# Scaling a GEMM's inputs one block earlier, and two more Winograd quads in that block

## The chip, the cores and the metric

One core of a Trainium2 chip. The metric is the device time of one execution in microseconds (us); the median of the runs counts.

## The reference

One transformer block on 256 tokens of width 2048, all in float32: a gated feed-forward stage (ffn), a mixer, and a second ffn.

```python
def _swiglu(x, w_gate, w_up, w_down):
    return (jax.nn.silu(x @ w_gate) * (x @ w_up)) @ w_down
...
        f = _swiglu(_rmsnorm(h, ln_ffn1_pre[l]), ffn1_gate[l], ffn1_up[l], ffn1_down[l])
        h = h + MACARON_WEIGHT * _rmsnorm(f, ln_ffn1_post[l])
        mx = _hybrid_mixer(_rmsnorm(h, ln_mix_pre[l]), ...)
        h = h + _rmsnorm(mx, ln_mix_post[l])
        f = _swiglu(_rmsnorm(h, ln_ffn2_pre[l]), ffn2_gate[l], ffn2_up[l], ffn2_down[l])
        h = h + MACARON_WEIGHT * _rmsnorm(f, ln_ffn2_post[l])
```

The feed-forward width is 5632, so gate and up are 2048 x 5632 each and down is 5632 x 2048. `_rmsnorm` divides each token's row by its root mean square: one factor per token (a row factor) and one gain per column.

## The kernel before

**Numbers in two halves.** Each float32 operand is split in a high half in a reduced format (a cast on ScalarE, ACT) and a low half, the rest (a subtraction on VectorE, DVE). A product is three matmuls (`mm3`, L317): high x high, high x low, low x high. Weights come from memory through SP's queue, two groups of 128 rows at a time (`w32`), and are split into a ring of five buffers (`wH`, `wL`): ACT line L295 and DVE line L296 where the framework orders the work, L373 and L383 where the kernel's own planner does.

**Gate and up.** Both have 11 blocks of 512 columns. Block 0 is made by `gemm_tok`, first gate, then up; the framework's scheduler places its instructions by program order and readiness, with the weight splits put ahead. Up of block 0 is 96 matmuls of 512 columns; its evacuation (`up(h)`: L1010, then a 32 x 32 block transpose, L875) is left to the plan that follows. Blocks 1 to 10 and the down stage are one plan: `Plan.solve` sorts all their operations by modelled times, due times and buffers, and the engines run them in that order. `p.begin` is a node of 12 us that stands for the last stretch of up of block 0; `UNITS` says how many of the 33 large buffers ("units") the plan may count on at its start.

**Pairs and quads.** A block is written as a string in `GATE_UP`. `f` is a pair: two groups of 128 input columns, all tokens, times gate's weights; `l` the same for up; a pair is 12 matmuls. `q` is a quad: two groups of input columns times both gate's and up's weights, by a Winograd form with seven products in place of eight (21 matmuls in place of 24). A quad costs seven VectorE operations on weights: L576 (two columns of 512 at once), L581 and L585 (512), and four low halves L598 (three of 1024, one of 512). It needs sums and differences of the inputs' halves (`sums`: four operations of 256 columns at L441 to L446, a cast at L482, a low half at L486; once for two quads). A block with quads ends in a merge: L640 on ACT, four adds L645, two closings L645, two totals L693 on VectorE.

**Row factors.** `uT` is the transposed input with the column gains, without the row factors `rs`. Block 0 and block 1 of before read `uT`, and their evacuation multiplies by `rs`. Blocks 2 to 10 read `nT`, which has the factors in it. `spread` turns `rs` from one number per partition into a row `rsb`: a copy on VectorE (L1099), a transpose on TensorE (L1101), a copy on ScalarE (L1102), once for each half of the tokens. `normed` then makes `nT` from `uT`, for four groups: join the halves (L1119), scale by `rsb` (L1123), cast the high half (ACT, L1132), subtract for the low half (L1127). In the kernel before these are operations of the plan; two joins run during up of block 0 and the rest during block 1. Block 1 has no quad; blocks 2, 4, 6, 8, 10 have four and blocks 3, 5, 7, 9 three.

**What else stands there.** `setup_mixer` (from `s.after`, first ffn only) loads the mixer's parameter rows by 12 small DMAs on SP and turns them on TensorE.

Of the kernel before, what the change touches and what calls it, by code (L numbers as in the profile page):

```python
# [10 lines left out]
F32 = mybir.dt.float32  # L11
F32R = mybir.dt.float32r
AF = mybir.ActivationFunctionType
ALU = mybir.AluOpType
# [3 lines left out]
P = 128  # L18
# [26 lines left out]
DOWN = ((0, "fffffffffffqfff" "qllqllqllqllqllqllqll", 0),  # L45
        (2, "fqflqfqflqfqflqfqflqfqfqff", TRAIL))
OUT = ((0, "", 0), (1, "fffqfq" "qlqlll", 0), (3, "", TRAIL))
GATE_UP = ["", "ffffffffllllllll"] + ["ffqfqfqlqlll", "fffqffqlqllll", "ffqfqfqlqlll", "fffqffqlqllll", "ffqfqfqlqlll", "fffqffqlqllll", "ffqfqfqlqlll", "fffqffqlqllll", "ffqfqfqlqlll"]
SUMS = (2, 2)
BY_DMA = range(0)  # L50
LAT = dict(PE=0.22, DVE=0.1, ACT=0.17, SP=0.0, POOL=8.0)
AGAIN = dict(PE=0.0, DVE=0.0, ACT=0.0, SP=0.0, POOL=0.0)
UNITS = dict(ffn=25, out=22)
FIFO = dict(pt=4, pm=4, tmp=TB)
SPARE, KEEP, URGENT, HOLD = 3, 4, 8.0, 99
SOON, FETCH, LATEST, BEFORE = 22.0, 22.0, 12.0, 12.0
EARLY = 0.5
NXSPARE = 1
RATE, LEAVE, LAND, ADD, MOVE = 0.28, 1.05, 2.0, 10.0, 12.0

ROWS = [("ln_mix_pre", 16), ("ln_ffn2_pre", 16), ("mu", 26), ("w0", 8), ("a0", 8),
# [5 lines left out]
def cost(eng, n, extra=0.0):  # L67
    return extra + (n / 960 + 0.068 if eng == "DVE" else n / 1200 + 0.095)
# [152 lines left out]
class Block:  # L221
# [99 lines left out]
        nc.tensor.matmul(ps, aL, bH, start=False, stop=stop)  # L321

    def gemm_tok(s, w, c0, at, KT, evac, lead=False, trail=False, xs=None, hold=False,
                 order=None):
        pss = [s.pm.tile([P, 512], F32, tag="mm", name=s.nm("mm")) for _ in range(2)]
        ws = {}

        def do(k, h):
            (wH, wL), (xH, xL) = ws[k], at(k)
            s.mm3(pss[h], xH[:, h * P:h * P + P], xL[:, h * P:h * P + P], wH, wL,  # L330
                  k == 0, k == KT - 1)

        def keep(tiles):
            ws.update((k, (wH, wL)) for k, wH, wL in tiles)

        def both(k0, k1):
            for k2 in order or range(k0, k1, 4):
                keep(s.load_w(w, k2, min(4, k1 - k2), c0, 512))
                for k in range(k2, min(k2 + 4, k1)):
                    do(k, 0)  # L340
                    do(k, 1)

        if trail:
            both(0, KT - TRAIL)
            s.by_half(w, c0, KT - TRAIL, KT, do, keep, lambda h, d: evac(h, d, lambda: pss[h]))
            return
        k0 = 0
        if xs:
            s.head(w, c0, KT, do, keep, xs)
            k0 = KT  # L350
        elif lead:
            s.by_half(w, c0, 0, STAG, do, keep, ready=s.ready)
            s.run()
            k0 = STAG
        both(k0, KT)
        if hold:
            return lambda h: evac(h, pss[h])
        with s.tc.high_priority(offset=BOOST):
            for h in range(2):
                evac(h, pss[h])  # L360
# [60 lines left out]
    def sums(s, T, Td, j, out, own=None, nq=2, used=(), x32=None):  # L421
# [11 lines left out]
            V.tensor_tensor(out=fl(x), in0=xH, in1=xL, op=ALU.add)  # L433

        def second():
            x = tt["x"] if x32 is None else x32[0][0].rearrange(
                "p (a b) t -> p a b t", b=2)[:, :nq]
            a11, a21 = x[:, :, 0, :P], x[:, :, 0, P:]
            a12, a22 = x[:, :, 1, :P], x[:, :, 1, P:]
            f = tt["f"] = s.unit((P, 4, nq, P), F32, "sf")  # L440
            V.scalar_tensor_tensor(out=f[:, 0], in0=a21, scalar=-1.0, in1=a22, op0=ALU.mult,  # L441
                                   op1=ALU.subtract)
            V.scalar_tensor_tensor(out=f[:, 1], in0=f[:, 0], scalar=-1.0, in1=a11,
                                   op0=ALU.mult, op1=ALU.subtract)
            V.tensor_tensor(out=f[:, 2], in0=a11, in1=a21, op=ALU.subtract)
            V.tensor_tensor(out=f[:, 3], in0=a12, in1=f[:, 1], op=ALU.subtract)  # L446

# [541 lines left out]
    def ffn(s, wg, wu, wd, uT, rs, gpost, resid, emit, reload, xs=None):  # L989
# [9 lines left out]
        def turned(b, h, src):  # L999
            if not T1[b]:  # L1000
                T1[b].append(s.unit(p="T1"))
            s.turn(T1[b][0], h, src)
# [5 lines left out]
        def ev_um(b, h, ps):  # L1008
            g = sig[b, h]
            nc.vector.scalar_tensor_tensor(out=g, in0=ps, scalar=rs[h], in1=g, op0=ALU.mult,  # L1010
                                           op1=ALU.mult)

        s.gemm_tok(wg, 0, at, NKD, lambda h, ps: ev_g(0, h, ps), lead=True, xs=xs)
        up = s.gemm_tok(wu, 0, at, NKD, lambda h, ps: (ev_um(0, h, ps), turned(
            0, h, sig[0, h])), hold=True)
        while s.after:
            s.after.pop(0)()
        rb = s.rtmp("rsb")
        s.spread(rs, rb)

        p = s.plan
        p.units = UNITS["ffn"]
# [13 lines left out]
            hTk.append(k)  # L1036
        carry(0, [last], k1)

        uTk = [Tok("unit") for _ in range(2 * len(uT))]
        for k in uTk:  # L1040
            k.of = "unit"
        nT, nTd, nTk, nx = s.normed(uT, rb)
        su, sud, suk = [None] * 4, {}, []

        def need(q):
            j = q // 2
            if j not in sud:
                sud[j], k = s.sums(nT, nTd, j, su, nq=SUMS[j], x32=nx[j])
                suk.extend(k)
            return sud[j]  # L1050

        for b in range(1, nb):
            mul, silu = {}, {}
            k1 = Tok("unit")

            def ev_f(h, d, ap, use, b=b, silu=silu):
                if b == 1:
                    before, mine = p.claim("tmp")
                    n = p.op("ACT", cost("ACT", 512, 0.05), lambda: ev_g(b, h, ap()),
                             [d] + before)  # L1060
                    silu[h] = n, mine
                    use.append(n)
                    return

                def f():
                    sig[b, h] = ap()
                    nc.scalar.activation(out=ap(), in_=ap(), func=AF.Silu)
                silu[h] = p.op("ACT", cost("ACT", 512), f, [d]), use

            def ev_l(h, d, ap, use, b=b, silu=silu, mul=mul, k1=k1):  # L1070
                g, mine = silu[h]

                def mult():
                    nc.vector.tensor_tensor(out=ap(), in0=ap(), in1=sig[b, h], op=ALU.mult)
                if b == 1:
                    m = p.op("DVE", one, lambda: ev_um(b, h, ap()), [d, g])
                    src, mine2 = (lambda: sig[b, h]), mine
                    use.append(m)
                else:
                    m = p.op("DVE", one, mult, [d, g])  # L1080
                    src, mine2 = ap, use
                    mine.append(m)
                t = p.op("DVE", one, lambda: turned(b, h, src()), [m],
                         [k1] if h == 0 else (), chain=f"turn{b}")
                mine2.append(t)
                mul[h] = t
            x, dep = (at, lambda k: None) if b == 1 else (s.T_at(nT), lambda k: nTd[k // 4])
            s.seven(wg, b * 512, wu, b * 512, x, dep, NKD, need, su, GATE_UP[b], ev_f, ev_l, {})
            if b == 1:
                p.release([p.last], uTk)  # L1090
            carry(b, [mul[0], mul[1]], k1)
        p.release([p.last], nTk + suk)
        s.post(wd, s.T_at(hT), NKF, gpost, 0.5, resid, emit, reload, hT, hTd, sm, DOWN, hTk)
# [9 lines left out]

    def normed(s, uT, rb):

        nc, p = s.nc, s.plan
        V = nc.vector
        nT = s.new_T(len(uT))
        fl = lambda t: t.rearrange("p k t -> p (k t)")
        done, toks, own = [], [], {}  # L1110
        rows = p.op("ACT", 2.0, lambda: None, [p.begin])
        for i in range(len(uT)):
            (uH, uL), (nH, nL) = uT[i], nT[i]
            x = {}
            kx, kT = Tok("unit"), [Tok("unit"), Tok("unit")]

            def join(x=x, uH=uH, uL=uL):
                x[0] = s.unit((P, 4, S), F32, "nx")
                V.tensor_tensor(out=fl(x[0]), in0=fl(uH).bitcast(F32), in1=fl(uL).bitcast(F32),  # L1119
                                op=ALU.add)  # L1120

            def scale(x=x):
                V.tensor_tensor(out=x[0], in0=x[0],  # L1123
                                in1=rb.unsqueeze(1).to_broadcast([P, 4, S]), op=ALU.mult)

            def low(x=x, nH=nH, nL=nL):
                V.tensor_tensor(out=fl(nL), in0=fl(x[0]), in1=fl(nH).bitcast(F32),  # L1127
                                op=ALU.subtract)
            n = p.op("DVE", cost("DVE", 1024), join, (), [kx], early=BEFORE - 3.0)
            n = p.op("DVE", cost("DVE", 1024), scale, [n, rows])  # L1130
            n = p.op("ACT", cost("ACT", 1024),
                     lambda x=x, nH=nH: nc.scalar.copy(fl(nH), fl(x[0])), [n], kT)  # L1132
            done.append(p.op("DVE", cost("DVE", 1024), low, [n], (),
                             () if i < len(SUMS) else [kx]))
            toks += kT
            if i < len(SUMS):
                own[i] = x, kx
        return nT, done, toks, own

    def post(s, wd, at, KT, gpost, fac, resid, emit, reload, hT, hTd, sm, plan, hTk=None):  # L1140
        nc = s.nc
# [873 lines left out]
```

## Time and profile before

| | |
|---|---|
| median of 3 runs | 2017.49 us (2016.72 to 2018.85) |
| the profiled execution's own time | 2017.13 us |
| its span, first to last instruction | 2015.4 us |
| TensorE clock granted | 0.998 |
| TensorE busy | 2000.9 us (99%) |
| weight loads into TensorE | 1655.1 us (82%) |
| VectorE busy | 1824.7 us (91%) |
| ScalarE busy | 1192.3 us (59%) |
| GpSimd busy | 327.6 us (16%) |

PE is TensorE, PEld its weight loads, DVE VectorE, ACT ScalarE, POOL GpSimd, SP the queue that issues most loads. In a table of stretches, each engine has its busy us and its number of instructions in brackets. In a timeline a row has start, duration, engine, line, operation, tiles (out<-in), shapes, count, and in brackets the idle time before it with what ended it. Matmul durations overlap (0.39 us each while they start 0.23 apart), and some matmul records can be missing.

The first ffn's gate/up runs from about 7 to 475 us of the span, the mixer from about 700 to 1230, the second ffn's gate/up from about 1310 to 1785.

### The profile page before, as it was taken

The numbers are of one execution on the slowest core, as the hardware profiler recorded it, in microseconds if no ns is written. First come the engines' busy times: TensorE is split into PE (matmuls) and PEld (weight loads), VectorE is DVE, ScalarE is ACT, GpSimd is POOL, SyncE is SP. The second block draws the span as 40 slices with busy tenths as digits, with TensorE's granted clock in tenths as the row PEclk, the third lists the DMA queues.
The fourth block names the chain that finished last, engine by engine and source line by source line (L and its number), as shares of the span: only waits on it lengthen the run. The fifth ranks groups of instructions, "written<-read, shape, count | busy, mean of one in ns | idle before, by whom it ended". The sixth has DMA issues, their size and how long they took to land.

```text
span 2015.4 us, 28684 instructions
## 1 busy us (share of the span) xinstructions
PE 2000.9 (99%) x9957; PEld 1655.1 (82%) x9957; DVE 1824.7 (91%) x2424; ACT 1192.3 (59%) x1586; POOL 327.6 (16%) x673
## 2 busy tenths in 40 slices
PE   9999999999999999999999999999999999999997
PEld 7888888888888888888788788888888888888886
DVE  6999999999999957789689678979999999999997
ACT  7555665556666566685476434665656555566663
POOL 0111211131000123403220111011113111310000
PEclk9999999999999999999999999999999999999999
DMA  7675674667568577757456547666656747665683
GB/s 268 224 241 182 220 242 160 218 213 241 175 203 299 209 212 214 205 175 214 146 173 190 159 168 269 244 216 215 228 198 218 245 142 235 211 228 183 207 294 126
DMA packets 227419, 423.56 MB, mean 210 GB/s; under 512 B 24639, under 2 KB 28105, under 8 KB 227273
## 3 DMA queue, kind: packets, MB, share of 16 engines
q1 hardware_dynamic: 204713, 384.70, 57.9%
q0 software_dynamic: 22272, 36.51, 5.5%
q8 instruction: 78, 1.28, 0.3%
q10 hardware_dynamic: 288, 0.52, 0.1%
q14 instruction: 68, 0.56, 0.1%
HBM read 396.69 MB, written 8.39 MB: 201 GB/s over the span
## 4 chain that ended last, share of the span: by engine, by line
PE 97%; DVE 1%; issue 1%; DMA 0%; ACT 0%; POOLq 0%; POOL 0%; DVEq 0%; ACTq 0%
PE mm L319 27%; PE mm L321 26%; PE mm L320 26%; PE ms L320 5%; PE ms L321 5%; PE ms L319 5%; PE tr L849 1%; PE pA L1733 0%; DVE u L645 0%; PE mc L817 0%; DMA x<-in_x_dram 0%; PE pU L1829 0%; PE pSa L1841 0%; PE pY L1864 0%; PE pT L1900 0%
## 5 line engine op out<-in xcount | busy, mean ns | idle before, releaser
L319 PE MATMUL mm<-wH,xH 128*128 128x512 f32 (+1 forms) x2116 | 825.5, 391 | 0.0
L320 PE MATMUL mm<-wL,xH 128*128 128x512 f32 (+1 forms) x2116 | 821.2, 388 | 0.0
L321 PE MATMUL mm<-wH,xL 128*128 128x512 f32 (+1 forms) x2116 | 821.1, 388 | 0.0
L319 PEld LDWEIGHTS mm<-wH,xH 128*128 128x128 f32 x2116 | 397.4, 188 | 82.1
L321 PEld LDWEIGHTS mm<-wH,xL 128*128 128x128 f32 x2116 | 397.4, 188 | 82.0 <-DVE xL L867 0.2
L373 ACT CAST wH<-w 128x1024 fp32r<-128x1024 f32 x313 | 326.2, 1054 | 231.7 <-PE mm L321 208.1
L320 PEld LDWEIGHTS mm<-wL,xH 128*128 128x128 f32 x2116 | 397.7, 188 | 79.7
L383 DVE TENSOR_TENSOR wL<-w,wH 128x1024 fp32r<-128x1024 f32 x313 | 373.0, 1218 | 18.9 <-ACT wH L373 17.3
L593 ACT CAST wH<-t 128x1024 fp32r<-128x1024 f32 x208 | 219.4, 1055 | 217.0 <-PE mm L321 108.9
L296 DVE TENSOR_TENSOR wL<-w,wH 128x1024 fp32r<-128x1024 f32 (+2 forms) x200 | 236.6, 1192 | 95.7 <-ACT wH L295 94.1
L295 ACT CAST wH<-w 128x1024 fp32r<-128x1024 f32 (+2 forms) x200 | 205.4, 1034 | 170.9 <-PE mm L321 150.7
L892 POOL DMA_DIRECT2D x<-T x352 | 173.1, 499 | 729.8 <-DVE T L875 190.3
L598 DVE TENSOR_TENSOR wL<-t,wH 128x1024 fp32r<-128x1024 f32 x208 | 248.6, 1217 | 0.7 <-ACT wH L593 0.7
L593 ACT CAST wH<-w 128x1024 fp32r<-128x1024 f32 x208 | 168.3, 835 | 56.6 <-PE mm L321 30.0
L598 DVE TENSOR_TENSOR wL<-w,wH 128x1024 fp32r<-128x1024 f32 x208 | 194.5, 951 | 0.3
L576 DVE TENSOR_TENSOR t<-w,w 128x1024 f32<-128x1024 f32 x104 | 126.7, 1218 | 0.0
L320 PE MATMUL ms<-wL,sH 128*128 128x512 f32 x276 | 107.6, 390 | 0.2
L319 PE MATMUL ms<-wH,sH 128*128 128x512 f32 x276 | 107.4, 389 | 0.0
L321 PE MATMUL ms<-wH,sL 128*128 128x512 f32 x276 | 107.4, 389 | 0.0
L585 DVE TENSOR_TENSOR t<-w,t 128x512 f32<-128x512 f32 x104 | 71.8, 690 | 2.6
L581 DVE TENSOR_TENSOR t<-w,t 128x512 f32<-128x512 f32 x104 | 71.3, 686 | 0.6
L645 DVE TENSOR_TENSOR u<-ms,u 128x512 f32<-128x512 f32 x92 | 61.4, 686 | 1.4
(317 smaller groups left out, 2107.8 us busy)
## 6 DMA issues: line engine op xcount, KB each, us to landing
w<-in_w_in_dram SPq DMA_DIRECT2D x128, 512.0 KB
w<-in_ffn_up_dram SPq DMA_DIRECT2D x112, 512.0 KB
w<-in_ffn_gate_dram SPq DMA_DIRECT2D x110, 512.0 KB
w<-in_ffn_down_dram SPq DMA_DIRECT2D x104, 512.0 KB
w<-in_ffn_down_dram SPq DMA_DIRECT2D x144, 256.0 KB
w<-in_ffn_gate_dram SPq DMA_DIRECT2D x132, 256.0 KB
w<-in_ffn_up_dram SPq DMA_DIRECT2D x128, 256.0 KB
w<-in_w_out_dram SPq DMA_DIRECT2D x24, 512.0 KB
```

Of the source, the lines that this page charges most:

```text
L295: s.nc.scalar.copy(vH, v)
L296: s.nc.vector.tensor_tensor(out=vL, in0=v, in1=vH.bitcast(F32), op=ALU.subtract)
L319: nc.tensor.matmul(ps, aH, bH, start=start, stop=False)
L320: nc.tensor.matmul(ps, aH, bL, start=False, stop=False)
L321: nc.tensor.matmul(ps, aL, bH, start=False, stop=stop)
L373: nc.scalar.copy(x["H"], x["v"])
L383: nc.vector.tensor_tensor(out=x["L"], in0=x["v"], in1=x["H"].bitcast(F32), op=ALU.subtract)
L576: V.tensor_tensor(out=v["t13"], in0=v["a"], in1=v["b"][:, :1].to_broadcast([P, 2, 512]), op=ALU.subtract)
L585: V.tensor_tensor(out=v["t24"][:, 1], in0=v["b"][:, 1], in1=v["t24"][:, 0], op=ALU.subtract)
L593: nc.scalar.copy(H, src)
L598: V.tensor_tensor(out=L, in0=src, in1=H.bitcast(F32), op=ALU.subtract)
L892: nc.gpsimd.dma_start(out=x[0][q * 32:q * 32 + 32, i], in_=src[i * 32:i * 32 + 32, q])
```

## The change

Row factors: `spread` and the joins now stand between gate and up of block 0, and `setup_mixer` after them, all ahead of up. Up's loop calls `aside` after each group of four; it writes scale, cast and low of one group of `nT` (`split`). `normed` has no plan operations any more; the plan takes `nT` as ready at `p.begin`, counts on 15 units in place of 25, and gets those of `uT` back at `p.begin` rather than after block 1. Block 1 reads `nT` like the others, with no factors in its evacuation.

Quads: block 1 gets two, and the strings of blocks 2 to 10 start with three, so that these hold 31 in place of 32: 33 per stage, not 32.

```diff
-GATE_UP = ["", "ffffffffllllllll"] + ["ffqfqfqlqlll", "fffqffqlqllll", "ffqfqfqlqlll", "fffqffqlqllll", "ffqfqfqlqlll", "fffqffqlqllll", "ffqfqfqlqlll", "fffqffqlqllll", "ffqfqfqlqlll"]
+GATE_UP = ['', 'fffffqfqllllll', 'fffqffqlqllll', 'ffqfqfqlqlll', 'fffqffqlqllll', 'ffqfqfqlqlll', 'fffqffqlqllll', 'ffqfqfqlqlll', 'fffqffqlqllll', 'ffqfqfqlqlll', 'fffqffqlqllll']
...
-UNITS = dict(ffn=25, out=22)
+UNITS = dict(ffn=15, out=22)
...
+JOINS = 4
...
     def gemm_tok(s, w, c0, at, KT, evac, lead=False, trail=False, xs=None, hold=False,
-                 order=None):
+                 order=None, aside=None):
...
                     do(k, 0)
                     do(k, 1)
+                if aside:
+                    aside(k2)
...
         s.gemm_tok(wg, 0, at, NKD, lambda h, ps: ev_g(0, h, ps), lead=True, xs=xs)
-        up = s.gemm_tok(wu, 0, at, NKD, lambda h, ps: (ev_um(0, h, ps), turned(
-            0, h, sig[0, h])), hold=True)
+        rb = s.rtmp("rsb")
+        nT, nx, join, split = s.normed(uT, rb)
+        s.spread(rs, rb)
+        for i in range(JOINS):
+            join(i)
         while s.after:
             s.after.pop(0)()
-        rb = s.rtmp("rsb")
-        s.spread(rs, rb)
+        up = s.gemm_tok(wu, 0, at, NKD, lambda h, ps: (ev_um(0, h, ps), turned(
+            0, h, sig[0, h])), hold=True, aside=lambda k: [
+                f(k // 4 + o) for f, o in ((split, 0), (join, JOINS)) if k // 4 + o < 4])
...
-        uTk = [Tok("unit") for _ in range(2 * len(uT))]
-        for k in uTk:
+        uTk, nTk = [[Tok("unit") for _ in range(2 * len(uT))] for _ in range(2)]
+        nxk = [Tok("unit") for _ in SUMS]
+        for k in uTk + nTk + nxk:
             k.of = "unit"
-        nT, nTd, nTk, nx = s.normed(uT, rb)
+        p.release([p.begin], uTk)
...
-                sud[j], k = s.sums(nT, nTd, j, su, nq=SUMS[j], x32=nx[j])
+                sud[j], k = s.sums(nT, [p.begin] * 4, j, su, nq=SUMS[j], x32=(nx[j], nxk[j]))
...
-            x, dep = (at, lambda k: None) if b == 1 else (s.T_at(nT), lambda k: nTd[k // 4])
-            s.seven(wg, b * 512, wu, b * 512, x, dep, NKD, need, su, GATE_UP[b], ev_f, ev_l, {})
-            if b == 1:
-                p.release([p.last], uTk)
+            s.seven(wg, b * 512, wu, b * 512, s.T_at(nT), lambda k: None, NKD, need, su,
+                    GATE_UP[b], ev_f, ev_l, {})
...
     def normed(s, uT, rb):
...
+        def join(i):
+            x[i] = s.unit((P, 4, S), F32, "nx")
+            V.tensor_tensor(out=fl(x[i]), in0=fl(uT[i][0]).bitcast(F32),
+                            in1=fl(uT[i][1]).bitcast(F32), op=ALU.add)
+
+        def split(i):
+            nH, nL = nT[i]
+            V.tensor_tensor(out=x[i], in0=x[i],
+                            in1=rb.unsqueeze(1).to_broadcast([P, 4, S]), op=ALU.mult)
+            nc.scalar.copy(fl(nH), fl(x[i]))
+            V.tensor_tensor(out=fl(nL), in0=fl(x[i]), in1=fl(nH).bitcast(F32),
+                            op=ALU.subtract)
+        return nT, x, join, split
```

The branches for block 1 in `ev_f` and `ev_l` (evacuation with the factors) go away, and block 1 takes the branch of the other blocks.

More of the change, by code (lines that the diff above doesn't have):

```diff
@@ L435, in second @@
         def second():
-            x = tt["x"] if x32 is None else x32[0][0].rearrange(
+            x = tt["x"] if x32 is None else x32[0].rearrange(
                 "p (a b) t -> p a b t", b=2)[:, :nq]
@@ L1056, in ev_f @@
             def ev_f(h, d, ap, use, b=b, silu=silu):
-                if b == 1:
[L1058 to L1063, printed above, removed]
                 def f():
@@ L1074, in mult @@
                     nc.vector.tensor_tensor(out=ap(), in0=ap(), in1=sig[b, h], op=ALU.mult)
[L1075 to L1083, printed above, removed]
+                m = p.op("DVE", one, mult, [d, g])
+                mine.append(m)
+                t = p.op("DVE", one, lambda: turned(b, h, ap()), [m],
                          [k1] if h == 0 else (), chain=f"turn{b}")
-                mine2.append(t)
+                use.append(t)
                 mul[h] = t
-            x, dep = (at, lambda k: None) if b == 1 else (s.T_at(nT), lambda k: nTd[k // 4])
-            s.seven(wg, b * 512, wu, b * 512, x, dep, NKD, need, su, GATE_UP[b], ev_f, ev_l, {})
-            if b == 1:
-                p.release([p.last], uTk)
+            s.seven(wg, b * 512, wu, b * 512, s.T_at(nT), lambda k: None, NKD, need, su,
+                    GATE_UP[b], ev_f, ev_l, {})
             carry(b, [mul[0], mul[1]], k1)
@@ L1104, in normed @@
     def normed(s, uT, rb):
-        nc, p = s.nc, s.plan
-        V = nc.vector
+        nc, V = s.nc, s.nc.vector
         nT = s.new_T(len(uT))
         fl = lambda t: t.rearrange("p k t -> p (k t)")
[L1110 to L1138, printed above, removed]
+        x = {}
+        def join(i):
[10 more added lines that the diff above has]
+        return nT, x, join, split
     def post(s, wd, at, KT, gpost, fac, resid, emit, reload, hT, hTd, sm, plan, hTk=None):
```

## The prediction

> **What bounds the kernel now.** I read the page's busy shares, then who TensorE waited for, then a table of stretches around gate/up, then single queues at the places the change touches.
>
> ```profile
> PE 2000.9 (99%) x9957; PEld 1655.1 (82%) x9957; DVE 1824.7 (91%) x2424; ACT 1192.3 (59%) x1586; POOL 327.6 (16%) x673
> ...
> PE 97%; DVE 1%; issue 1%; DMA 0%; ACT 0%; POOLq 0%; POOL 0%; DVEq 0%; ACTq 0%
> ```
> ```profile
> engine line waited for: us in total, times, longest us
> PE warm L725 <- POOL ident masks.py:199: 1.7, 1, 1.7
> PE tr L849 <- DMA x<-in_x_dram: 1.2, 1, 1.2
> PE pU L1829 <- DVE R L1854: 0.3, 1, 0.3
> ```
> ```profile
> core 0: us, PE busy (x) PEld busy (x) DVE busy (x) ACT busy (x) POOL busy (x), PEclk, DMA share, GB/s
> 33.40:55.30 21.90, 21.90 (x99) 18.09 (x98) 15.27 (x20) 14.85 (x23) 1.09 (x2) 1.00 0.90 297
> 55.30:98.90 43.60, 43.60 (x195) 36.07 (x194) 41.70 (x46) 24.67 (x28) 8.07 (x16) 1.00 0.65 220
> 98.90:470.00 371.10, 371.10 (x1639) 307.29 (x1638) 366.69 (x418) 221.05 (x246) 70.72 (x144) 1.00 0.64 212
> 1341.00:1362.80 21.80, 21.80 (x98) 18.06 (x97) 13.42 (x14) 10.75 (x11) 0.00 (x0) 1.00 0.87 298
> 1362.80:1406.00 43.20, 43.20 (x193) 35.71 (x193) 41.28 (x47) 24.66 (x28) 7.93 (x16) 1.00 0.63 213
> 1406.00:1778.00 372.00, 372.00 (x1643) 308.14 (x1642) 367.50 (x418) 221.03 (x246) 70.69 (x144) 1.00 0.64 212
> ```
> The chain of waits is TensorE itself for 97%. Of its three listed waits two lie at the very start and one in the mixer; none lies in either gate/up stage. The table has, for each ffn, up of block 0, block 1, and blocks 2 to 10 (up to the last few us). TensorE is busy in every microsecond of all six rows. So in gate/up time is a number of matmuls times their spacing. VectorE is the second limit: 41.70 of 43.60 us in block 1, 366.69 of 371.10 in blocks 2 to 10, but only 15.27 of 21.90 and 13.42 of 21.80 in up of block 0.
>
> **TensorE's part.** One matmul every 0.227 us: eight starts with seven steps from the first row below to the last (1.59 us), and 371.10 us over x1639 gives 0.226.
>
> ```profile
> 99.71 0.39 PE L321 MATMUL mm<-wH,xL 128*128 128x512 f32 x1
> ...
> 101.30 0.39 PE L319 MATMUL mm<-wH,xH 128*128 128x512 f32 x1
> ```
> A quad does with seven products (three matmuls each) what two pairs do with eight. The strings in GATE_UP hold 32 quads before (4,3,4,3,4,3,4,3,4) and 33 after (2 in block 1, then 3,4,3,4,3,4,3,4,3). One product less per stage, two stages: 2 x 3 x 0.227 = **1.36 us less**. All of it lies on the path. The two transposes of `spread` (L1101) only change their place in TensorE's queue.
>
> **VectorE's part.** Back to back, operations start this far apart:
>
> ```profile
> 70.23 1.22 DVE L1119 TENSOR_TENSOR nx<-xH,xL 128x1024 f32<-128x1024 f32 x1
> 71.36 1.22 DVE L383 TENSOR_TENSOR wL<-w,wH 128x1024 fp32r<-128x1024 f32 x1
> ...
> 97.39 0.68 DVE L909 TENSOR_TENSOR xL<-x,xH 128x512 fp32r<-128x512 f32 x1
> 97.99 1.22 DVE L576 TENSOR_TENSOR t<-w,w 128x1024 f32<-128x1024 f32 x1
> ```
> So 1.13 to 1.14 us for 1024 columns, 0.60 for 512. Per stage: a quad costs 4 x 1.14 + 3 x 0.60 = 6.4, a pair 1.14; one quad for two pairs is +4.1. Block 1 had no merge and now has one: four adds (L645), two closings, two totals, 8 x 0.60 = +4.8. The twelve operations of `normed` (join, scale, low, four each) stay twelve but go to block 0; two joins were there already, so 10 x 1.14 = 11.4 us move.
>
> Block 1 then has on VectorE 41.7 - 11.4 - 4.6 (four pairs) + 12.7 (two quads) + 4.8 - 2.6 (the second group of sums, priced below, now first needed in block 2) = 40.6 us in a block of 42.2. It fits, with 1.6 us over. Blocks 2 to 10 lose one quad, 4.1 us less. ScalarE, at 14.85 of 21.90 us in up of block 0, takes four more copies of about 1.05, which fits.
>
> **The seam between block 0 and block 1** is the doubtful place. VectorE there, first ffn:
>
> ```profile
> 40.66 0.36 DVE L1099 COPY rb<-rs 128x128 f32<-128x128 f32 x2
> ...
> 44.17 1.23 DVE L296 TENSOR_TENSOR wL<-w,wH 128x1024 fp32r<-128x1024 f32 x1 [2.02 <-ACT wH L295]
> 45.89 1.23 DVE L383 TENSOR_TENSOR wL<-w,wH 128x1024 fp32r<-128x1024 f32 x1 [0.50 <-ACT wH L373]
> ...
> 54.05 1.23 DVE L383 TENSOR_TENSOR wL<-w,wH 128x1024 fp32r<-128x1024 f32 x1 [0.36 <-ACT wH L373]
> 55.20 0.75 DVE L1010 SCALAR_TENSOR_TENSOR sg<-mm,rs,sg 128x512 f32<-128x512 f32 x1
> ...
> 80.44 0.42 DVE L441 SCALAR_TENSOR_TENSOR sf<-nx 128x256 f32<-128x256 f32 x1
> ...
> 81.91 1.22 DVE L383 TENSOR_TENSOR wL<-w,wH 128x1024 fp32r<-128x1024 f32 x1
> ```
> ```profile
> 41.93 1.27 ACT L1006 ACTIVATE sg<-mm,rs 128x512 f32<-128x512 f32 x2
> ```
> ```profile
> L1101 PE MATMUL rb<-ident,rb x6: 270/272/273, 55.5 to 1363.2; 128*128 128x128 f32 x6
> ```
> ```profile
> L1102 ACT COPY rsb<-rb x6: 253/264/275, 56.6 to 1364.4; 128x128 f32<-128x128 f32 x6
> ```
> 6.6 us idle, 11.4 us more to do: VectorE comes to block 1 about 4.8 us late. The cover: four weight halves of block 1 (L383, the first and the last of four in the rows) are finished when TensorE begins it, each good for 12 x 0.227 = 2.72 us, 10.9 us in all. If scale and low stand before all of them: the row factors are spread by about 43.5 (copy rb at 40.66 to 41.0, transposes of 0.27, then two copies L1102 on ScalarE, 0.26 each, behind the gate's two evacuations, which end at 43.2), the last weight half of up and eight operations end at about 43.5 + 9 x 1.14 = 53.8, the first L383 at 54.9. Block 1 begins at about 55.5, where the transposes of `spread` stand in the trace of before. So no wait, by 0.6 us. By the first quad (five pairs later, 69.1) VectorE must do five weight halves (5.7), up's evacuation (4 x 0.60), the first sums (1.5, from 80.44 to 81.91 in the rows, and 1.14), two operations of the quad (2.3): 53.8 + 13.0 = 66.8, with 2 us to spare. From there each pair gives back 2.72 - 1.14 us. In the second ffn VectorE has more idle time (8.4 us). Bounds of the seam: nothing, to 4.8 us per stage if no cover counted. I take nothing, nearest to the rows of cover.
>
> **The transposes.** In the trace of before those of ffn 1 stand behind up; now they stand inside it. The mixer shows that place already:
>
> ```profile
> 719.67 0.22 DVE L1099 COPY rb<-rs 128x128 f32<-128x128 f32 x1
> ...
> 719.38 0.62 PE L319 MATMUL mm<-wH,xH 128*128 128x512 f32 x2
> 719.84 0.27 PE L1101 MATMUL rb<-ident,rb 128*128 128x128 f32 x1
> 719.87 0.48 PE L320 MATMUL mm<-wL,xH 128*128 128x512 f32 x1
> ```
> The matmul behind the transpose starts at once, so nothing is lost there; I take 0.
>
> **The loads moved ahead.** `setup_mixer` (first ffn only) now stands before up: its 12 small loads pass up's first four on SP.
>
> ```profile
> 13.57 3.75 SPq L281 DMA_DIRECT2D w<-in_ffn_up_dram  x4
> 17.69 0.33 SPq L1307 DMA_DIRECT2D cols<-in_ln_mix_pre_dram  x1
> ...
> 28.10 0.29 SPq L1307 DMA_DIRECT2D cols<-in_pool_scale_dram  x1
> 31.42 4.95 SPq L281 DMA_DIRECT2D w<-in_ffn_up_dram  x4
> ```
> ```profile
> 36.26 1.06 ACT L295 CAST wH<-w 128x1024 fp32r<-128x1024 f32 x1
> ```
> They take 10.7 us of the queue, so up's first load would go out at 24.3. From the issue at 31.42 to that load's cast at 36.26 are 4.8 us; so cast at 29.1, split by 31.4, needed at 55.5 - 96 x 0.227 = 33.7. Hidden, with 2.3 us over; if all slots moved to 28.4, 1.8 us late, once. I take 0.
>
> **Sum.** The profiled execution took 2017.13 us (span 2015.4 and 1.7 around it), 0.36 under the median of 2017.49. 2017.13 - 1.36 = 2015.8; on the median **2016.1**. About 0.2% (4 us) is what a measurement of this kernel can tell from no change, so this counts as no change.
>
> **A rule against this reading.** The Trainium skill, "Perfetto Trace Analysis", section "Identifying the Most-Contended Engine", says that TensorE's matmul busy share does not tell how near its limit it is; the weight loads' share does, and the engine with the highest occupancy is the one to work on. Here PEld has 82% and the rule would name VectorE. The trace disagrees as far as the path goes: TensorE lists no wait in these stages.
>
> **Rivals.**
> 1. VectorE sets the pace of blocks 1 to 10 (the reading which that rule suggests): it is busy 408.4 of 414.7 us there, and its work changes by 4.1 + 4.8 - 11.4 = -2.5 us per stage: 2017.5 - 5.0 = 2012.5, faster. Against it: no wait of TensorE on VectorE. 0.04.
> 2. The gain is eaten, as if the change did nothing: VectorE's spare 0.6, 2 and 1.6 us in block 1 don't all hold, and TensorE waits 0.7 to 2.7 us per stage. 2016.1 + 1.4 to 5.4 is 2017.5 to 2021.5. For it: block 1 gets VectorE's densest work just when its cover is thin. 0.22.
> 3. Slower: the two transposes keep their place behind up, as in the trace of before. Then the factors come at 57, and block 1, which now reads the scaled inputs from its first matmul (second group of four), waits for scale, copy and low of two groups, 4 x 1.14 and some: to about 61.9 instead of 55.5, 6.3 us per stage: 2016.1 + 12.6 = 2028.7. It decides from the point where the factors come later than about 44. Against it: `spread` is now written before up, and the mixer's case. 0.06.
> 4. Slower: VectorE's 4.8 us at the seam all become waits: 2016.1 + 9.6 = 2025.7. It decides once the chain of scales ends after 54.4. Against it: the 10.9 us of cover. 0.10.
>
> **How the numbers follow.** Forecast 0.58, at 2016.1, between 2014.5 and 2017.5 (the runs shown scatter by 2.1 us). Faster by over 0.2% (under 2013.5): rival 1, 0.04. Within: forecast and rival 2, 0.80. Slower (over 2021.5): rivals 3 and 4, 0.16. The range from 2014.5 to 2021.5 leaves out 0.04 and 0.16.
>
> **What would show it.** Right: L319 to L321 have six matmuls fewer, each spaced 0.227, TensorE stays busy in all six stretches, the rb transposes lie some 40 matmuls into up, and VectorE in up of block 0 goes to nearly full with the first L383 of block 1 at about 54 to 55 us. Wrong: a wait of TensorE on `xL` (scale chain, rival 3), on `wL` L383 at the start of block 1 (rival 4), on `wL` L598 or `sL` at the first quads (rival 2), on L296 at the start of up (the moved loads), or block 1 shorter by more than 1.4 us (rival 1).

## The result, and the profile after

The changed kernel takes 2021.71 us (median of 14 runs, 2021.23 to 2024.25) where the kernel before takes 2017.13 (14 runs, 2016.56 to 2018.85): ratio 1.0023, 95% interval 1.0015 to 1.0032, about 4.6 us slower. The profiled execution has a span of 2020.1 us against 2015.4, at the same granted clock of 0.998.

The page's busy shares and its chain of waits, after:

```profile
PE 2000.9 (99%) x9951; PEld 1652.0 (82%) x9951; DVE 1839.2 (91%) x2450; ACT 1196.6 (59%) x1592; POOL 326.3 (16%) x673
...
PE 90%; DVE 5%; DMA 2%; issue 2%; ACT 0%; SPq 0%; DVEq 0%; POOLq 0%; POOL 0%; ACTq 0%
```

TensorE has six matmuls fewer, as the strings say. VectorE is busy 14.5 us longer, and 5% of the chain where it had 1%. Whom TensorE waited for, after:

```profile
PE warm L728 <- POOL ident masks.py:199: 1.7, 1, 1.7
PE mm L320 <- ACT wH L296: 1.5, 1, 1.5
PE pA L1710 <- DVE R L1686: 1.3, 2, 1.1
PE pB L1729 <- DVE R L1721: 1.0, 2, 0.8
PE mm L322 <- DVE xL L870: 0.7, 2, 0.5
PE tr L852 <- DMA x<-in_x_dram: 0.7, 1, 0.7
PE mm L320 <- ACT sgb L1346: 0.6, 1, 0.6
PE ms L321 <- DVE wL L601: 0.4, 1, 0.4
```

New are one wait of 1.5 us in gate of block 0, and three in the mixer, 2.9 us together, whose text the change does not touch. Two smaller ones are new as well: `xL` at 7.9 and 9.5 us, where gate begins, and `wL` L601 at 590 us, in the first ffn's down stage. None lies at up of block 0 or at the second ffn's gate/up. The stretches, after (columns as before), and behind them before's row for the first stretch:

```profile
core 0: us, PE busy (x) PEld busy (x) DVE busy (x) ACT busy (x) POOL busy (x), PEclk, DMA share, GB/s
0.00:33.40 33.40, 28.82 (x134) 22.34 (x135) 23.07 (x49) 22.80 (x53) 3.08 (x34) 1.00 0.72 254
33.40:55.30 21.90, 21.90 (x101) 18.12 (x100) 19.38 (x27) 17.82 (x28) 1.08 (x2) 1.00 0.66 218
55.30:98.90 43.60, 43.56 (x192) 35.74 (x191) 43.36 (x50) 24.03 (x27) 8.05 (x16) 1.00 0.95 332
...
1362.80:1406.00 43.20, 43.20 (x193) 35.76 (x192) 41.54 (x47) 23.67 (x27) 7.88 (x16) 1.00 0.91 318
```
```profile
0.00:33.40 33.40, 30.44 (x142) 25.06 (x143) 21.44 (x49) 22.72 (x52) 3.09 (x34) 1.00 0.73 260
```

To place the loss, here is when TensorE reaches certain matmuls, read from the timelines: before in us from the start of the span, and how much later (+) or earlier each kernel gets there. A row's steps show where time is lost. The experiments e1 to e11 follow below.

| | gate, 49th matmul | down of ffn 1 | mixer, first pn | mixer, first pb | last turn ahead of ffn 2 | down of ffn 2 | span |
|---|---|---|---|---|---|---|---|
| before | 21.60 | 499.10 | 856.17 | 917.05 | 1326.23 | 1806.70 | 2015.43 |
| after | -0.3 | +1.2 | +1.9 | +5.5 | +5.5 | +4.8 | +4.7 |
| e1 | -0.3 | -0.3 | -0.2 | -0.3 | -0.3 | -1.0 | -0.9 |
| e2 | +0.1 | +1.7 | +1.7 | +5.3 | +5.2 | +5.2 | +5.2 |
| e3 | +0.4 | +4.0 | +3.9 | +7.6 | +7.5 | +6.8 | +7.0 |
| e4 | +0.4 | +3.4 | +3.4 | +3.4 | +3.3 | +4.1 | +4.1 |
| e5 | 0.0 | +0.8 | +1.0 | +0.9 | +0.9 | +0.2 | +0.2 |
| e6 | +0.6 | +1.3 | +1.3 | +4.9 | +4.9 | +5.6 | +5.6 |
| e7 | -0.4 | +0.3 | +0.3 | +0.2 | +0.2 | +0.9 | +0.9 |
| e8 | -0.2 | -0.2 | -0.2 | +3.4 | +3.4 | +2.9 | +2.9 |
| e9 | +1.1 | +2.6 | +2.5 | +2.6 | +2.5 | +3.4 | +3.8 |
| e10 | +0.2 | +1.2 | +1.2 | +1.2 | +1.1 | +0.6 | +0.7 |
| e11 | -0.1 | +0.8 | +0.8 | +0.9 | +0.8 | +1.1 | +1.4 |

After: 1.5 us lost between the first gate and the first down, 0.7 from there to pn, 3.6 between pn and pb in the mixer, and 0.7 won in the second ffn's gate/up. In the 0.7 ahead of pn lies the 0.4 us wait at 590 us; e2, whose first ffn has the same text, loses nothing there, and the cause stays open. What varies ahead of the 49th matmul is the start: when the first loads land, and how soon matmuls start 0.23 us apart (in before they are 0.43 apart up to 9.65 us).

**The 1.5 us in gate.** VectorE's timeline in the last part of gate, before and after:

```profile
24.80 1.13 DVE L867 SCALAR_TENSOR_TENSOR xL<-tr,g,xH 128x128 fp32r<-128x128 f32 x4 [0.95 <-ACT xH L858]
25.84 1.22 DVE L296 TENSOR_TENSOR wL<-w,wH 128x1024 fp32r<-128x1024 f32 x1
28.00 1.13 DVE L867 SCALAR_TENSOR_TENSOR xL<-tr,g,xH 128x128 fp32r<-128x128 f32 x4 [0.94 <-ACT xH L858]
```
```profile
24.48 1.12 DVE L870 SCALAR_TENSOR_TENSOR xL<-tr,g,xH 128x128 fp32r<-128x128 f32 x4 [0.95 <-ACT xH L861]
25.52 3.48 DVE L1105 TENSOR_TENSOR nx<-xH,xL 128x1024 f32<-128x1024 f32 x3
28.92 1.22 DVE L297 TENSOR_TENSOR wL<-w,wH 128x1024 fp32r<-128x1024 f32 x1
30.06 1.12 DVE L870 SCALAR_TENSOR_TENSOR xL<-tr,g,xH 128x128 fp32r<-128x128 f32 x4
```

Three joins (L1105), written behind gate, run in the middle of it, as soon as their input groups are turned; gate's weight subtraction moves from 25.84 to 28.92. TensorE, after:

```profile
27.69 0.40 PE L320 MATMUL mm<-wH,xH 128*128 128x512 f32 x1
29.57 0.73 PE L320 MATMUL mm<-wH,xH 128*128 128x512 f32 x2 [1.48 <-ACT wH L296]
30.19 0.50 PE L321 MATMUL mm<-wL,xH 128*128 128x512 f32 x1
```

The wait is put down to a cast on ScalarE, but L321 with the low half starts at 30.19, about when the late subtraction ends (28.92 + 1.22 = 30.14); two matmuls that need no low half were ordered ahead of it. From 27.69 to 30.19 are 2.50 us, in which three matmuls start; at 0.227 each they need 0.68, so by matmul starts 1.8 us are lost here. With 0.3 more at 76 us in block 1 and 0.7 less for the product, that comes to about the 1.5 us of the table.

**The 3.6 us in the mixer.** ScalarE at the same place, after and before:

```profile
867.14 0.62 ACT L296 CAST wH<-w 128x512 fp32r<-128x512 f32 x1 [1.97 <-PE mm L322]
867.66 0.36 ACT L1653 COPY R<-pV 64x256 f32<-64x256 f32 x1
...
868.95 0.51 ACT L1331 ACTIVATE zb<-R,cols 128x256 f32<-128x256 f32 x1
```
```profile
863.19 0.51 ACT L1354 ACTIVATE zb<-R,cols 128x256 f32<-128x256 f32 x1
...
866.63 0.62 ACT L295 CAST wH<-w 128x512 fp32r<-128x512 f32 x1
867.15 0.37 ACT L1676 COPY R<-pV 64x256 f32<-64x256 f32 x1
```

Before, six shift activations (L1354; L1331 after) run first and then a cast and copies that depend on TensorE. After, the cast and the copies stand ahead, ScalarE sits idle 1.97 us for TensorE, and the first activation comes 5.8 us later, 3.9 more than the mixer's own +1.9. VectorE's operations behind it feed pA and pB, where TensorE waits. The engines run another order, on unchanged text. From about 730 to 1185 us VectorE and ScalarE have just two orders in all the traces of this document: before's in before, e1, e4, e5, e7, e9, e10 and e11, after's in after, e2, e3, e6 and e8.

### The profile page after: what moved, and what is told of

Same layout as the page of the kernel before. It is cut to its first block, busy times and chain, and to the rows that moved or that the text cites. A ratio compares the mean times of both kernels' runs of the same rounds, so it can differ in the third digit from the quotient of the medians.

```text
span 2020.1 us, 28729 instructions
## 1 busy us (share of the span) xinstructions
PE 2000.9 (99%) x9951; PEld 1652.0 (82%) x9951; DVE 1839.2 (91%) x2450; ACT 1196.6 (59%) x1592; POOL 326.3 (16%) x673
## 4 chain that ended last, share of the span: by engine, by line
PE 90%; DVE 5%; DMA 2%; issue 2%; ACT 0%; SPq 0%; DVEq 0%; POOLq 0%; POOL 0%; ACTq 0%
PE mm L320 25%; PE mm L321 24%; PE mm L322 24%; PE ms L321 4%; PE ms L322 4%; PE ms L320 4%; DMA w<-in_ffn_down_dram 1%; DVE wL L386 1%; DVE wL L601 1%; PE tr L852 0%; DVE t L579 0%; DMA w<-in_ffn_up_dram 0%; PE pA L1710 0%; DMA w<-in_ffn_gate_dram 0%; DVE xL L912 0%
## 5 line engine op out<-in xcount | busy, mean ns | idle before, releaser
L321 PE MATMUL mm<-wL,xH 128*128 128x512 f32 (+1 forms) x2104 | 816.9, 388 | 0.0
L321 PEld LDWEIGHTS mm<-wL,xH 128*128 128x128 f32 x2104 | 395.1, 188 | 80.5 <-DVE wL L297 0.9
L386 DVE TENSOR_TENSOR wL<-w,wH 128x1024 fp32r<-128x1024 f32 x309 | 367.9, 1215 | 10.0 <-ACT wH L376 8.4
L596 ACT CAST wH<-t 128x1024 fp32r<-128x1024 f32 x212 | 223.6, 1055 | 216.1 <-PE mm L322 122.2
L601 DVE TENSOR_TENSOR wL<-t,wH 128x1024 fp32r<-128x1024 f32 x212 | 253.4, 1215 | 1.8 <-ACT wH L596 1.8
L601 DVE TENSOR_TENSOR wL<-w,wH 128x1024 fp32r<-128x1024 f32 x212 | 197.5, 949 | 0.2
L321 PE MATMUL ms<-wL,sH 128*128 128x512 f32 x282 | 109.9, 390 | 0.4 <-DVE wL L601 0.4
L648 DVE TENSOR_TENSOR u<-ms,u 128x512 f32<-128x512 f32 x100 | 66.8, 685 | 1.5
```

Of the source, the lines that this page charges most:

```text
L321: nc.tensor.matmul(ps, aH, bL, start=False, stop=False)
L386: nc.vector.tensor_tensor(out=x["L"], in0=x["v"], in1=x["H"].bitcast(F32), op=ALU.subtract)
L596: nc.scalar.copy(H, src)
L601: V.tensor_tensor(out=L, in0=src, in1=H.bitcast(F32), op=ALU.subtract)
```

## The experiments

Line numbers of these kernels differ from those of after by a few; e6 and e7 have before's. Unless said otherwise, mixer and second ffn are as in after.

**e1 and e2: the change in one ffn only.**

```diff
-        s.ffn_old(ffn1_gate[0], ffn1_up[0], ffn1_down[0], uT, rs, ln_ffn1_post[0],
+        s.ffn(ffn1_gate[0], ffn1_up[0], ffn1_down[0], uT, rs, ln_ffn1_post[0],
...
-        s.ffn(ffn2_gate[0], ffn2_up[0], ffn2_down[0], uT3, rs3, ln_ffn2_post[0],
+        s.ffn_old(ffn2_gate[0], ffn2_up[0], ffn2_down[0], uT3, rs3, ln_ffn2_post[0],
```

(from e1 to e2; `ffn_old` is the stage of before.)

> The change in the second ffn only, the first ffn as before. Theory A (the loss is three separate things: each gate/up stage gains 0.65 us; three joins stand ahead of gate's last weight splits in the first ffn, +1.9; the mixer's ScalarE order, settled by what comes before it, +3.6): the mixer's order is that of before, so 2017.1 - 0.7 = 2016.5. Theory B (the new plan of gate/up is itself slower, VectorE being too full, alike in both stages): half of the loss, 2019.4.

> The change in the first ffn only. Theory A: all of the loss and one stage's gain, 2021.7 + 0.65 = 2022.4. Theory B: half of the loss, 2019.4.

e1: 2016.40 us beside 2016.88 for before, ratio 0.9998 (0.9989 to 1.0007). e2: 2022.11, ratio 1.0026 (1.0017 to 1.0036). Both as theory A has it, though e1's interval alone does not tell its gain from no change. In the table e1 has before's mixer and wins 0.7 in the second ffn's gate/up, three matmuls at 0.227; e2 has all of the loss, the mixer's 3.6 too.

**e3: the first ffn's joins written behind gate's last split.**

```diff
             s.stats()
+            s.joins()
...
-        for i in range(JOINS):
-            join(i)
```

(the first place is gate's head, where the order is fixed by hand.)

> The changed kernel with the first ffn's four joins written behind the last weight split of gate's head, in its fixed order; nothing else. Theory A: gate no longer waits, 2021.7 - 1.9 = 2019.8, the mixer as slow as in the changed kernel. Theory B: no change, 2021.7.

2024.16, ratio 1.0038 (1.0024 to 1.0052): a miss. The wait did not go; it moved and grew. TensorE's waits in e3:

```profile
PE mm L321 <- DVE wL L297: 1.9, 1, 1.9
...
PE mm L321 <- DVE wL L386: 1.1, 1, 1.1
```

Four joins in a row now hold up the first weight half behind the head, and a half in block 1 comes late too. This points to a lack of room on VectorE, with the place of the joins deciding where it shows; e5 tries a third place.

**e4: the quads of blocks 2 to 10 in another sequence.**

```diff
-'fffqffqlqllll', 'ffqfqfqlqlll', 'fffqffqlqllll', 'ffqfqfqlqlll', 'fffqffqlqllll', ...
+'fffqffqlqllll', 'ffqfqfqlqlll', 'fffqffqlqllll', 'ffqfqfqlqlll', 'ffqfqfqlqlll', ...
```

(from 3,4,3,4,3,4,3,4,3 to 3,4,3,4,4,3,4,3,3 quads.)

> The changed kernel with its 33 quads in another order of blocks (2, then 3,4,3,4,4,3,4,3,3 in place of 3,4,3,4,3,4,3,4,3); the framework then orders the mixer on VectorE, ScalarE and TensorE exactly as in the kernel before. Theory A: the mixer's 3.6 us go, the joins' 1.9 stay: 2018.1. Theory B: the same number of quads and of VectorE operations, 2021.7.

2020.87, ratio 1.0020 (1.0012 to 1.0029). The mixer's part came true: +3.4 at pn and at pb. The rest did not: in the timeline TensorE loses another 1.3 to 1.5 us in each gate/up stage, in pieces of 0.3 us or less that the list of waits does not show, each at or right behind a matmul with a weight's low half, behind the two adjacent blocks of four quads (about 325 to 405 us, and again in ffn 2).

**e5: the first ffn's joins one by one, between the steps of gate's head.**

```diff
+HEAD_JOINS = {4: 0, 6: 1, 8: 2, 10: 3}
...
                     split(k + 4)
+                    if k in HEAD_JOINS:
+                        s.join(HEAD_JOINS[k])
```

> The changed kernel with the first ffn's joins written into gate's head one by one, each behind a weight split, where VectorE stood idle about 0.95 us per step in the kernel before; the framework then orders VectorE and ScalarE in the mixer as in the kernel before. Theory A: the joins' 1.9 us and the mixer's 3.6 us go, both stages' gain stays: 2016.9 - 1.3 = 2015.6. Theory C (after the run with all joins behind the head: VectorE has no room for the joins before the row factors are known, wherever they stand): the wait comes back, at gate's end or at up's first splits, 2017.0 to 2019.0.

2017.38 beside 2017.15, ratio 1.0001 (0.9992 to 1.0010): in the span of C, but at neither of the places that C named. Gate's wait is gone and the mixer is before's, but TensorE now waits in block 1. VectorE and TensorE there, in e5:

```profile
72.58 1.22 DVE L580 TENSOR_TENSOR t<-w,w 128x1024 f32<-128x1024 f32 x1
73.83 0.69 DVE L585 TENSOR_TENSOR t<-w,t 128x512 f32<-128x512 f32 x1
74.44 1.22 DVE L387 TENSOR_TENSOR wL<-w,wH 128x1024 fp32r<-128x1024 f32 x1
```
```profile
75.71 0.50 PE L322 MATMUL mm<-wL,xH 128*128 128x512 f32 x1 [1.11 <-DVE wL L387]
```

Behind the first quad VectorE still makes the second quad's weights when the next pair's low half is due.

**e6 and e7: before, with 31 quads in place of 32.** Two sequences of strings, chosen because the build of one gives the mixer the order that after has, and the other before's:

```diff
 (quads in blocks 2 to 10)
-before 4,3,4,3,4,3,4,3,4
+e6     3,4,3,4,3,4,3,4,3
+e7     4,3,4,3,4,3,3,3,4
```

> The kernel before with one quad less per stage (blocks 2 to 10 with 3,4,3,4,3,4,3,4,3) and nothing else; the framework then orders VectorE and ScalarE in the mixer as in the changed kernel. Theory A: 2016.9 + 1.4 (one product per stage) + 3.6 (the mixer) = 2021.9. Without the mixer's part: 2018.3.

> The kernel before with one quad less per stage in another place (4,3,4,3,4,3,3,3,4); the framework orders the mixer as in the kernel before. Theory A: 2016.9 + 1.4 = 2018.3. If the mixer's order were nothing, the same as the run beside it with 3,4,3,4,3,4,3,4,3.

e6: 2022.42 beside 2017.15, ratio 1.0027 (1.0017 to 1.0037). e7: 2018.44, ratio 1.0005 (0.9996 to 1.0014). Both as expected. Neither holds any of the change's code. The mixer's loss in e6 is the same as after's, with the same waits:

```profile
PE pA L1733 <- DVE R L1709: 1.2, 2, 1.0
PE pB L1752 <- DVE R L1744: 1.1, 2, 0.8
PE mm L319 <- ACT sgb L1369: 0.6, 1, 0.6
```

And the traces of both show the price of a product from the other side: one more per stage costs 0.7 us in each ffn, although VectorE has, by the prediction's prices, 4.1 us less to do there.

**e8, e9, e10, e11: as e5, with block 1's quads placed later.**

```diff
-e5  'fffffqfqllllll'
+e8  'ffffffqlqlllll'
+e9  'ffffffqllqllll'
+e10 'fffffqflqlllll'
+e11 'ffffffqlllqlll'
```

> As the kernel with the joins between gate's steps, and block 1's second quad one pair later (ffffffqlqlllll); the framework then orders the mixer as in the changed kernel. Theory A: 3.6 us above the run with the mixer's order of before, 2019.2. If the mixer's order were nothing: the same as that run.

> The kernel with the joins between gate's steps, and block 1's second quad two pairs later (ffffffqllqllll); the framework orders VectorE and ScalarE in the mixer as in the kernel before. Theory A with VectorE's lateness at the seam: the 1.5 us that TensorE waited at block 1's first quads in the run with the joins between the steps go too, so both stages' gain is left over: 2017.1 - 1.4 = 2015.7. Theory C (the lateness is a matter of VectorE's sum up to the end of block 1, wherever the quads stand): the wait moves to the second quad, 2017.2.

> As joins between the head's steps (four joins one by one between gate's weight splits), with block 1's second quad one pair later (fffffqflqlllll in place of fffffqfqllllll); its mixer has before's order of instructions. Theory A (the change is worth -0.68 us per gate/up stage, and the wait of 1.3 us at 74 us is only the second quad coming too early for a late VectorE): that wait goes, no other comes, the mixer is as before, 2015.8 beside a before of 2017.1 (ratio 0.9993). Theory C (VectorE has no room for the moved work in the first ffn's blocks 0 and 1, wherever the quad stands, so a wait of 1 to 2 us turns up at a neighbouring place): 2016.8 to 2017.8, ratio about 1.000.

> As joins between the head's steps, with block 1's first quad one pair later and its second quad three pairs after it (ffffffqlllqlll); the mixer has before's order of instructions on VectorE and ScalarE. Theory A (the 1.3 us wait at 74 us comes from a first quad that starts before the late VectorE has caught up, as the run with ffffffqlqlllll had no such wait): no wait over 0.3 us in either gate/up stage, second gate/up again 0.5 to 0.7 us shorter, the mixer as before, 2015.9 to 2016.4 beside a before of 2017.1 (ratio about 0.9995). Theory C (the plan has no room on VectorE, and a later quad only moves the wait): waits of 0.4 to 1.3 us in blocks 1 to 6 of the stages, 2017.0 to 2019.5.

e8: 2020.02, ratio 1.0015 (1.0006 to 1.0024); e9: 2020.83, 1.0016 (1.0007 to 1.0026); e10: 2017.52, 1.0001 (0.9992 to 1.0010); e11: 2018.57, 1.0008 (0.9999 to 1.0017). Theory A was missed by e9, e10 and e11, and e8 came 0.8 above it; theory C held in e10 and e11, and e9 missed both. (The expectations of e8 and e9 name the second quad only; by the strings the first comes one pair later too.) With both quads one pair later (e8) nothing over 0.3 us is waited for in block 1, and the stage comes out as long as before, with 0.7 us won and about as much lost in small pieces; this build's mixer has after's order, so e8 as a whole is slower. With only the second quad later (e10) the wait of 1.1 us stays: it is the half behind the first quad that is late. With the first one pair later and the second three (e11) 0.3 us of it stay in block 1 and the rest moves on: by the timeline 0.8 us are lost at 276 us and 0.7 at 1584, in block 6 of both ffns. e11's and e10's waits:

```profile
PE mm L322 <- DVE wL L387: 1.4, 3, 0.6
```
```profile
PE mm L322 <- DVE wL L387: 1.1, 1, 1.1
```

e9's profiled execution also had a low clock in part of its first 20 us, which accounts for some of its first column in the table; behind that, it loses 1.5 us in ffn 1 and 0.9 in ffn 2, with listed waits of 0.4 us at 234 and 1543 us:

```profile
0.00:10.00 10.00, 6.72 (x26) 4.66 (x26) 2.92 (x9) 4.75 (x12) 3.08 (x34) 0.91 0.75 266
10.00:20.00 10.00, 10.00 (x47) 8.06 (x47) 7.23 (x18) 6.62 (x17) 0.00 (x0) 0.92 1.05 386
```

These two clocks are means: from 8.2 to 11.6 us it was 0.50, and 1.00 on both sides.

No version was shown to beat before. e1 is the nearest to it, and its interval holds no change.

## Why the prediction was wrong, step by step

The forecast was 2016.1 us, the runs give 2021.7, just outside the range. Its mechanism, a product less at no other cost, held in one of the two stages. Three steps failed: the mixer was taken as unchanged, the joins were reckoned into up of block 0, and the seam was reckoned only to block 1's first quad.

**TensorE's part** was right: six matmuls fewer, 0.7 us per stage. e1's trace shows it alone, those of e6 and e7 show the same price with the other sign.

**The term left out: the mixer's order.** The sum took everything outside gate/up as unchanged, without a word on it; only its text is. It is 3.6 us, most of the loss. From pn to pb TensorE takes 60.9 us in before and 64.5 in after, and each of the eleven experiments has one of the two: 60.8 to 61.0 in seven, 64.5 in e2, e3, e6 and e8. e6 against e7 (4.0 us between the medians, 3.6 of it from pn to pb) shows that neither the moved scaling nor block 1's quads are needed for it. What turns it is open: the framework orders the mixer with all that it placed earlier in hand, and the runs show two outcomes, not the rule that picks one. Moving instructions inside the mixer by hand to settle that was not tried.

**The joins' place** was the failed step of the VectorE sum. The prediction let up of block 0 hold all twelve operations and counted idle time from 33.4 on. The joins need no row factors, so three ran at 25.5 in gate, where VectorE had 0.95 us of idle time at each step. That made the weight half 3.1 us later (28.92 against 25.84), more than TensorE had in reserve. Price: 1.8 us by matmul starts, and it was in no rival.

**The seam**: it held in the second ffn. In the first, the factors came later than the 43.5 that was worked out, and scale and low did not stand ahead of all of block 1's weight halves, as was assumed: the first of these (L386) runs at 51.04. The transposes and VectorE's rows, after:

```profile
L1093 PE MATMUL rb<-ident,rb x6: 270/272/273, 44.4 to 1353.2; 128*128 128x128 f32 x6
```
```profile
45.20 4.63 DVE L1110 TENSOR_TENSOR nx<-nx,rsb 128x1024 f32<-128x1024 f32 x4
...
51.04 1.21 DVE L386 TENSOR_TENSOR wL<-w,wH 128x1024 fp32r<-128x1024 f32 x1
52.18 2.35 DVE L1113 TENSOR_TENSOR xL<-nx,xH 128x1024 fp32r<-128x1024 f32 x2
54.45 1.22 DVE L386 TENSOR_TENSOR wL<-w,wH 128x1024 fp32r<-128x1024 f32 x1
55.58 2.35 DVE L1113 TENSOR_TENSOR xL<-nx,xH 128x1024 fp32r<-128x1024 f32 x2
```

The eight operations end at 57.9; without the two weight halves between them (2 x 1.14) that is 55.6, against 53.8 worked out, 1.8 late. In e5, where gate has no wait, the scales still start at 44.83 us, so most of this is not due to that wait. This eats most of the 2 us to spare at the first quad, and the reckoning stopped there, with two of the quad's seven operations: a whole quad takes 6.4 us of VectorE and 21 x 0.227 = 4.8 of TensorE, so it takes 1.6 us where a pair gives 1.6 back, and only one pair stands between the first quad and the second, whose weights come due at once. VectorE's 40.6 us for block 1 came out as 43.36, some 2.4 of it the end of the eight operations. After shows little wait there, 0.04 us of idle time in block 1 (0.3 by matmul starts), since TensorE had come 1.5 us later out of gate; e5 takes that away and 1.1 us turn up in block 1. Rival 2 (the gain is eaten; VectorE's small margins don't all hold) therefore names the mechanism for the first ffn, where 1.5 us are lost instead of 0.7 won, a swing of 2.2 inside its 0.7 to 2.7; it is wrong for the second, where nothing is lost. Without the mixer's 3.6 the time would have been about 2018.1, in its span of 2017.5 to 2021.5.

**The transposes** kept no place behind up (rival 3): 44.4 and 1353.2, 41 and about 28 matmuls into up, where some 40 were foretold. **The moved loads** cost nothing, and for another reason than the slack that was reckoned: they did not pass up's first loads. SP's queue, after:

```profile
13.09 3.77 SPq L282 DMA_DIRECT2D w<-in_ffn_up_dram  x4
17.24 0.33 SPq L1284 DMA_DIRECT2D cols<-in_ln_mix_pre_dram  x1
```

**Rival 4** (all 4.8 us of VectorE's lateness become waits, in each stage) has the right sign and the wrong place: no weight half at the start of block 1 was waited for. **Rival 1** (VectorE sets the pace) is false as it was put: no stage got shorter than its matmuls, and e6 and e7, with less work for VectorE, get slower by a product per stage. Still VectorE, 43.36 us busy of 43.60 in block 1, is so near its limit that e3, e5, e9, e10 and e11 each found a wait of 0.4 to 1.9 us by moving its work about, and e4 lost as much in small pieces. The Trainium skill's rule, in "Perfetto Trace Analysis", section "Identifying the Most-Contended Engine", to work on the engine with the highest occupancy, would have named VectorE (91%) if TensorE is judged by its weight loads (82%), as the prediction did; the section names, beside these, the matmul work done against the peak, which was not worked out here. The runs agree with it in so far as VectorE decides whether a product saved on TensorE is kept, and not in that it sets the time.

## What to carry to other kernels

Where a scheduler orders instructions at build time, compare the order of the parts that a change does not touch as well: here they cost more than the part that was changed. An operation is placed by what it depends on, not only by where it is written; ask for each moved one from when it could run, and what stands behind it there. And a second engine at 98% makes every saving on the first conditional: reckon its lateness to the point where it next has idle time, not to the first deadline.

## What the runs showed that was not expected

The same mixer in two instruction orders takes 60.9 or 64.5 us from pn to pb, with nothing between, over thirteen kernels. And a mean clock can hide a short dip: one profiled execution (e9) had a granted clock of 0.50 from 8.2 to 11.6 us and 1.00 from there up to the last 10 us, where every run's falls. A table by stretches shows this as 0.91 and 0.92, the page's mean as 0.997.
